# Raw weight tiles in the empty places of the next block's tokens, and roots of the norms on VectorE, in a hybrid decoder step

## Chip, cores and metric

One core of a Trainium2 chip runs the whole step. The metric is the device time of one execution in microseconds; the time before is the median of three runs.

## What is computed

One layer for 2048 prompt tokens and 64 sample tokens (8 sequences of 8) with D = 1024. The sample tokens attend to a paged cache of 8192 positions each. Cut to what matters here:

```python
h = rmsnorm(x, norm1_g)
b, c, u, q, k, v = project(h, w_in)
y_conv, new_conv = short_conv(b, c, u, conv_state, conv_w)
o = attend(q, k, v, lam)
...
x = x + jnp.concatenate([y_conv, o], axis=-1) @ w_out
h2 = rmsnorm(x, norm2_g)
x = x + jnp.square(jax.nn.relu(h2 @ w_up)) @ w_down
...
y_prompt = rmsnorm(xp, final_g)
y_sample = rmsnorm(xs, final_g)
```

`rmsnorm` divides by the root of a row's mean square. Everything is float32; a product is made of three matmuls on high and low parts.

## The kernel before

Five instruction streams are written in one program order by hand; each engine works through its own part of it in that order, and SP's and GpSimd's queues issue transfers in order too. There are three stages: the input projection (to about 640 us), the prompt's attention with the convolution and the first output projection (to about 1180 us), and the stage that the change is about: output projection and MLP. The decode attention of the sample tokens (gathers of `kraw` and `vpg` on GpSimd's queue, transposes `kt` on VectorE, small matmuls) is dealt out in steps between the matmuls until about 2640 us.

In the third stage the prompt's tokens come in four blocks of 384 (`Dense` objects in `ds`, three tiles of 128 tokens each), and a fifth block holds the 64 sample tokens and the last 512 prompt tokens in five tiles. `Dense.run` (L1454) works through one block: the first four up chunks (`first_ups`), then a loop over `c`: a down product of two weight tiles (`down`, L1400), a `poll()`, and two up chunks (`up`, L1377), each followed by a `poll()`. There are NC = 16 such chunks. Near the end it calls the next block's `out_proj` (L1313 is its add of x) between its last two down products, so that blocks overlap. `poll` (L2085) takes one entry from the list `rest`; `before_last` empties that list and loads the mixed activations of the next block.

Weights stream through `Weights` (L204): `load` issues a tile of 512 KB into a raw buffer `wr` of two; `split` makes `wh` on ScalarE (L227) and `wl` on VectorE (L229), four buffers each, and then loads the next raw tile. So two raw tiles are on their way, and a raw load is issued when the one two before it has been split. TensorE reads `wh` and `wl` alone.

Tokens of block i stand in three places `x1_(i mod 2)0..2` of the pool `xb`. They are read from HBM by `load_x` (L1243), get both residual adds there (L1313, L1418), and leave by `final` (L1441). So the three places of the other parity are empty from the last `final` of a block to the next `load_x` into them. In the kernel before, the second block's tokens are loaded by the first polls of the first block on SP's queue; those of the third and fourth block by the polls after a block's outputs, on GpSimd's queue.

Norms: `norm_sum` (L272) squares and sums a row on ScalarE (`junk`, L277). `norm_root` (L280) makes the root in ten steps on one column, two of them integer steps that always run on VectorE (L287, L288), the others on the engine that is passed. `Dense` passes `self.eng`, which EN1 and ENG set to GpSimd. It is used in `norm_early` (L1273), in front of `scale` (which makes `xn`, L1256) and `turn` (tps, h2h, h2l), and in `final` (in front of y, L1450), where GpSimd's queue also sends y out. The first output projection, inside attention, passes GpSimd by itself (L1692). In the input projection `prep_root` (L357) does the same for three rows at once by `rsqrt` (L137), and L474 passes GpSimd.

Of the kernel before, what the change touches and what calls it, by code (L numbers as in the profile page):

```python
# [8 lines left out]
F32 = mybir.dt.float32  # L9
# [9 lines left out]
P = 128  # L19
# [2 lines left out]
LAM0 = 0.8 - 0.6  # L22
RATES = (0.8, 0.45, 0.8)
BURST = (3, 2, 1, 0)
ENG = True
MO = (5, 2, 1, 0, 0)
ST = 0
OW = 3
# [21 lines left out]
KUP = True  # L50
DA = 2
SHR = 0
EN1 = True
DW = 20.0
GP2 = (2, 1, 2, 3, 2, 2, 3, 3)
GP = (3, 2, 1, 3, 2, 2, 3, 3)
# [6 lines left out]
NDS = 4  # L63
# [4 lines left out]
def tile_hymba_step(  # L68
# [7 lines left out]
    nc = tc.nc  # L76
# [127 lines left out]
    class Weights:  # L204


        def __init__(self, pool, srcs, raw_bufs, bufs, share=0):
            self.share = share
            self.pool, self.srcs, self.rb, self.b = pool, srcs, raw_bufs, bufs
            self.raw, self.out, self.nr, self.ns, self.ng = {}, {}, 0, 0, 0  # L210
            self.parts_left = 0

        def load(self, upto):
            while self.nr < min(upto, len(self.srcs)):
                src = self.srcs[self.nr]
                t = self.pool.tile([P, 1024], F32, tag="wr", bufs=self.rb, name="wraw")
                dma(out=t.rearrange("p (k f) -> p k f", k=src.shape[1]), in_=src)
                self.raw[self.nr] = t
                self.nr += 1

        def split(self, upto):
            while self.ns < min(upto, len(self.srcs)):
                self.load(self.ns + 1)
                t = self.raw.pop(self.ns)
                wh = self.pool.tile([P, 1024], F32R, tag="wh", bufs=self.b, name="wh")
                wl = self.pool.tile([P, 1024], F32R, tag="wl", bufs=self.b, name="wl")
                nc.scalar.copy(wh, t)  # L227
                eng = nc.gpsimd if self.share and dec["gen"] is not None and self.ns % self.share == 1 else nc.vector
                eng.tensor_sub(wl, t, wh.bitcast(F32))  # L229
                k = self.srcs[self.ns].shape[1]  # L230
                self.out[self.ns] = (wh.rearrange("p (k f) -> p k f", k=k), wl.rearrange("p (k f) -> p k f", k=k))
                self.ns += 1
                self.load(self.ns + self.rb)

        def parts(self):

            if self.ns == len(self.srcs):
                return []
            i, box = self.ns, {}
            self.ns += 1  # L240
            self.parts_left = 4
            self.load(i + 1)

            def high(h):
                if h == 0:
                    box["t"] = self.raw.pop(i)
                    box["h"] = self.pool.tile([P, 1024], F32R, tag="wh", bufs=self.b, name="wh")
                    box["l"] = self.pool.tile([P, 1024], F32R, tag="wl", bufs=self.b, name="wl")
                nc.scalar.copy(box["h"][:, 512 * h:512 * h + 512], box["t"][:, 512 * h:512 * h + 512])
                self.parts_left -= 1  # L250

            def low(h):
                c = slice(512 * h, 512 * h + 512)
                nc.vector.tensor_sub(box["l"][:, c], box["t"][:, c], box["h"][:, c].bitcast(F32))
                self.parts_left -= 1
                if h == 1:
                    k = self.srcs[i].shape[1]
                    self.out[i] = tuple(box[x].rearrange("p (k f) -> p k f", k=k) for x in "hl")
                    self.load(i + 1 + self.rb)

            return [lambda: high(0), lambda: high(1), lambda: low(0), lambda: low(1)]

# [88 lines left out]
    def prep_stats(bi, ci):  # L351
        ss = prep_sums(bi, ci)
        for i in range(len(chunks[bi][ci])):
            prep_sum(bi, ci, ss, i)
        return ss

    def prep_root(bi, ci, ss, eng=None):  # L357
        rr = small.tile([P, 8], F32, tag="nrr", name="rr")
        w = len(chunks[bi][ci])
        nc.vector.tensor_scalar(ss[:, 0:w], ss[:, 0:w], EPS, None, op0=ALU.add)  # L360
        rsqrt(rr, ss, P, w, eng)
        return rr

    def prep_scale(bi, ci, rr):

        def f(i):
            x, n = xt[bi, ci][i], chunks[bi][ci][i][2]
            nc.vector.scalar_tensor_tensor(x[:n], x[:n], rr[:n, i:i + 1], g1[:n], op0=ALU.mult, op1=ALU.mult)
        return [lambda i=i: f(i) for i in range(len(chunks[bi][ci]))]
# [75 lines left out]
    cs = {}  # L445

    class Proj:


        def __init__(self, bi, mi):  # L450
# [20 lines left out]
            if mi == len(order) - 8 and bi + 1 < len(blocks):  # L471
                prep_load(bi + 1, 0)
            if mi == len(order) - 6 and bi + 1 < len(blocks):
                cs["scale"] = prep_scale(bi + 1, 0, prep_root(bi + 1, 0, prep_stats(bi + 1, 0), nc.gpsimd))  # L474
            if bi == 0 and mi == 8:
                cs["consts"] = conv_consts()
            if bi == 0 and mi == 10:
# [634 lines left out]
    for j in range(1, 4 * H):  # L1112
        h, g = divmod(j, 4)
# [47 lines left out]
    NC = NF // CH  # L1161
# [27 lines left out]
    class Dense:  # L1189
# [261 lines left out]
                                               op0=ALU.mult, op1=ALU.mult)  # L1451
                eng.dma_start(out=dst[r0:r0 + n, :], in_=y[:n])

        def run(self, ub, poll, before_last, nxt, after):  # L1454
            self.ub = ub
            self.first_ups()
            for c in range(NC - 2):
                self.down(range(c * CH, (c + 1) * CH))
                poll()
                ms = range((c + 2) * CH, (c + 3) * CH)  # L1460
                if c < NC - 3:
                    for m in ms:
                        self.up(m)
                        poll()
            w = []
            if len(self.groups) == 1 and KUP:

                w = [W.get() for m in ms]
                pss = [psA.tile([P, 512], F32, tag="a", name="ups")[:, 0:self.nt] for m in ms]
                for g in range(2):  # L1470
                    for i in range(len(ms)):
                        if 2 * g + i == HU:
                            dec["hold"] = True
                        self.up_rows(pss[i], w[i], 0, range(4 * g, 4 * g + 4))
                        if i == 0:
                            W.ahead(1 + g)
                    before_last(g)
                for ps, m in zip(pss, ms):
                    self.up_out(ps, m, 0)
                W.ahead(WL)  # L1480
            else:

                for gi in range(len(self.groups)):
                    for i, m in enumerate(ms):
                        if gi == 0:
                            w.append(W.get())
                            W.ahead(2)
                        self.up_chunk(m, gi, w[i])
                W.ahead(3)
            if after is None:  # L1490
                self.down(range((NC - 2) * CH, (NC - 1) * CH))
                nxt().out_proj()
                self.down(range((NC - 1) * CH, NF))
            else:
                self.down(range((NC - 2) * CH, NF), after)
# [569 lines left out]
    dec["paused"] = False  # L2065
    burst(BURST[1])
    box = {}
    rest = [lambda ti=ti: ds[1].load_x(ti) for ti in range(3)]

    def switch():  # L2070

        if box or dec["gen"] is not None:
            return
        dec["close"]()
        dctx.close()
        sm = ctx.enter_context(tc.tile_pool(name="mlp_sm", bufs=1, side="right", reuse_waits="tile"))
        slots = xslots(NDS) + [(sm, f"x1_{ti}") for ti in range(3, 5)]
        t0 = 384 * NDS
        d = Dense([[(xs, ys, 0, NS)] + ptiles(t0, t0 + 256), ptiles(t0 + 256, T)], sm, slots, ENG and nc.gpsimd)
        box["d"] = d  # L2080
        box["todo"] = [lambda gi=gi, x=x, g=g: d.load_mix(gi, [g], x)
                       for gi in range(2) for g in range(2) for x in "hl"]
        box["todo"] += [lambda ti=ti: d.load_x(ti) for ti in list(range(3, 5)) + list(range(3))]

    def poll():  # L2085
        switch()
# [5 lines left out]
    def before_last(g):  # L2092
        while rest:
            rest.pop(0)()
        if cur[0] < NDS - 1:
            ds[cur[0] + 1].load_mix(0, [g])
            return
        drain()
        switch()
        while box["todo"]:  # L2100
            box["todo"].pop(0)()

    cur = [0]
    for i, d in enumerate(ds):
        cur[0] = i
        d.run([(sb1, "uh", "ul", 4, 384)], poll, before_last, lambda: ds[cur[0] + 1] if cur[0] < NDS - 1 else box["d"], None)
        rest += [lambda: load_gain("f", nc.gpsimd)] + FN * [lambda: None]
        for ti in range(4):
            rest += [lambda d=d, ti=ti: d.final(ti, nc.gpsimd), lambda: None]
        if i < NDS - 1:  # L2110
            rest.append(lambda: load_gain("2", nc.gpsimd))
        if i < NDS - 2:
            rest += [lambda i=i, ti=ti: ds[i + 2].load_x(ti, nc.gpsimd) for ti in range(3)]
    c1.close()
    psA = ctx.enter_context(tc.tile_pool(name="mlp_psA2", bufs=8, space=PSUM, reuse_waits="tile"))
    sb2 = ctx.enter_context(tc.tile_pool(name="mlp_sb2", bufs=1, reuse_waits="tile"))
# [37 lines left out]
```

## Time and profile before

| what | value |
|---|---|
| time, median of three runs (lowest to highest) | 3207.14 us (3206.44 to 3207.63) |
| the profiled execution | 3218.23 us, of it the span 3216.5 us |
| busy share of the span | TensorE 95%, VectorE 59%, ScalarE 41%, GpSimd 28% |
| DMA | 624.7 MB, mean 194 GB/s |

The span is counted from the first to the last instruction. The page cuts it into 40 slices: TensorE is at nine tenths or more in nearly all from the third on, and its granted clock shows nine tenths or more in every slice. The DMA digits are highest, 5 to 8, where decode and MLP run together, and 2 after decode has ended.

### The profile page before, as it was taken

To read this page: it belongs to the slowest core of one execution; us is meant where nothing else is said; L and a number is where in the kernel's file an instruction comes from. 1 tells how busy PE (TensorE), PEld (TensorE's weight loads), DVE (VectorE), ACT (ScalarE), POOL (GpSimd) and SP (SyncE) were. 2 spreads that over 40 slices of the span, in tenths; PEclk is the share of its full clock that TensorE was granted. 3 is DMA by queue.
4 is the path that set the end of the run, shared out by engine and by line. 5 is a ranking of instruction groups with operands and counts; after the bars stand their busy time and mean duration, and the time that the engine had idled before them with its cause. 6 is when DMAs were issued, how large, how long until landed. Compare 5 with 4: busy or idle time off the path is not lost.

```text
span 3216.5 us, 55392 instructions
## 1 busy us (share of the span) xinstructions
PE 3046.2 (95%) x21670; PEld 2597.1 (81%) x21670; DVE 1905.9 (59%) x3861; ACT 1334.1 (41%) x2873; POOL 896.5 (28%) x1274
## 2 busy tenths in 40 slices
PE   7998998999999999998999999999989999999998
PEld 7997877989997888876777767777767888788887
DVE  5465344268888667765667656666556554454454
ACT  3323323357778643342343424333333433333333
POOL 1012353311222120133554344544335430110001
PEclk9999999999999999999999999999999999999999
DMA  5666875854335356676787786787757756232222
GB/s 156 220 222 217 287 255 164 258 142 111 105 102 147 128 169 209 221 233 236 249 284 271 239 289 220 258 285 267 279 189 254 230 181 201 74 101 81 79 79 76
DMA packets 443295, 624.74 MB, mean 194 GB/s; under 512 B 36661, under 2 KB 337717, under 8 KB 426650
## 3 DMA queue, kind: packets, MB, share of 16 engines
q1 hardware_dynamic: 378730, 335.68, 33.9%
q0 software_dynamic: 63136, 282.11, 24.8%
q8 instruction: 171, 2.80, 0.4%
q10 hardware_dynamic: 1168, 3.41, 0.3%
q14 instruction: 90, 0.74, 0.1%
HBM read 565.35 MB, written 55.74 MB: 193 GB/s over the span
## 4 chain that ended last, share of the span: by engine, by line
PE 74%; DVE 8%; issue 5%; DMA 5%; ACT 4%; POOL 3%; another core or an unknown queue 1%; SPq 0%; ACTq 0%; POOLq 0%; DVEq 0%
PE ups L200 7%; PE ups L202 7%; PE ups L201 6%; PE dps L1411 6%; PE dps L1412 6%; PE dps L1413 6%; PE ps L200 6%; PE ps L202 5%; PE ps L201 5%; PE asc L1833 3%; PE o_ps L950 3%; PE sps L903 3%; PE O L1920 3%; DMA wraw<-in_w_out_dram 2%; DVE kt L718 2%
## 5 line engine op out<-in xcount | busy, mean ns | idle before, releaser
L229 DVE TENSOR_TENSOR wl<-wraw,wh 128x1024 fp32r<-128x1024 f32 x408 | 498.3, 1222 | 325.5 <-ACT wh L227 245.4
L227 ACT CAST wh<-wraw 128x1024 fp32r<-128x1024 f32 x408 | 425.7, 1049 | 578.7 <-PE dps L1413 179.6
L708 POOL DMA_INDIRECT vpg<-in_cache_v_dram,pt x512 | 537.7, 1050 | 329.5 <-PE o_ps L950 155.4
L200 PE MATMUL ups<-h2h,wh 128*128 128x384 f32 (+2 forms) x1520 | 503.9, 332 | 9.7 <-DVE x L1418 7.7
L202 PE MATMUL ups<-h2h,wl 128*128 128x384 f32 (+2 forms) x1520 | 490.8, 323 | 1.0 <-DVE wl L229 1.0
L201 PE MATMUL ups<-h2l,wh 128*128 128x384 f32 (+2 forms) x1520 | 489.3, 322 | 0.1
L1412 PE MATMUL dps<-wl,uh 128*128 128x512 f32 (+1 forms) x1076 | 428.1, 398 | 26.2 <-DVE wl L229 24.8
L1411 PE MATMUL dps<-wh,uh 128*128 128x512 f32 (+1 forms) x1076 | 439.3, 408 | 9.6 <-DVE x L1313 3.4
L1418 DVE TENSOR_TENSOR x<-dps,x 128x512 f32<-128x512 f32 (+1 forms) x534 | 355.5, 680 | 136.3 <-PE dps L1413 120.3
L1413 PE MATMUL dps<-wh,ul 128*128 128x512 f32 (+1 forms) x1076 | 425.1, 395 | 0.0
L200 PE MATMUL ps<-hh,wh 128*128 128x384 f32 (+1 forms) x1152 | 406.0, 352 | 2.7 <-issue 1.6
L202 PE MATMUL ps<-hh,wl 128*128 128x384 f32 (+1 forms) x1152 | 377.2, 327 | 3.1 <-DVE wl L229 2.5
L201 PE MATMUL ps<-hl,wh 128*128 128x384 f32 (+1 forms) x1152 | 377.2, 327 | 1.2 <-issue 1.1
L700 POOL DMA_INDIRECT kraw<-in_cache_k_dram,idxk x128 | 127.3, 994 | 862.3 <-DVE kt L718 824.9
L1370 DVE TENSOR_TENSOR ul<-r,uh 128x384 fp32r<-128x384 f32 (+2 forms) x190 | 100.3, 528 | 385.3 <-ACT uh L1369 350.2
L200 PEld LDWEIGHTS ups<-h2h,wh 128*128 128x128 f32 x1520 | 286.4, 188 | 45.1 <-issue 38.0
L718 DVE STREAM_TRANSPOSE kt<-kraw 128x512 f32<-128x512 f32 x512 | 317.7, 677 | 0.0
L201 PEld LDWEIGHTS ups<-h2l,wh 128*128 128x128 f32 x1520 | 286.7, 189 | 2.3
L202 PEld LDWEIGHTS ups<-h2h,wl 128*128 128x128 f32 x1520 | 286.1, 188 | 2.2 <-DVE wl L229 1.8
L1367 ACT ACTIVATE r<-ups 128x384 f32<-128x384 f32 (+2 forms) x190 | 88.2, 464 | 440.6 <-PE ups L202 341.5
L1411 PEld LDWEIGHTS dps<-wh,uh 128*128 128x128 f32 (+1 forms) x1076 | 201.3, 187 | 80.9 <-issue 26.5
L1412 PEld LDWEIGHTS dps<-wl,uh 128*128 128x128 f32 (+1 forms) x1076 | 201.9, 188 | 72.6 <-DVE wl L229 34.4
(275 smaller groups left out, 4843.4 us busy)
## 6 DMA issues: line engine op xcount, KB each, us to landing
wraw<-in_w_up_dram SPq DMA_DIRECT2D x160, 512.0 KB
wraw<-in_w_down_dram SPq DMA_DIRECT2D x160, 512.0 KB
wraw<-in_w_in_dram SPq DMA_DIRECT2D x72, 512.0 KB
wraw<-in_w_out_dram SPq DMA_DIRECT2D x40, 512.0 KB
x<-in_x_prompt_dram SPq DMA_DIRECT2D x21, 512.0 KB
vpg<-in_cache_v_dram,pt POOLq DMA_INDIRECT x512
qt<-QH SPq DMA_DIRECT2D x64, 128.0 KB
qt<-QL SPq DMA_DIRECT2D x64, 128.0 KB
```

Of the source, the lines that this page charges most:

```text
L200: nc.tensor.matmul(ps, lhsT=wh, rhs=ah, start=first, stop=False)
L201: nc.tensor.matmul(ps, lhsT=wh, rhs=al, start=False, stop=False)
L202: nc.tensor.matmul(ps, lhsT=wl, rhs=ah, start=False, stop=last)
L227: nc.scalar.copy(wh, t)
L229: eng.tensor_sub(wl, t, wh.bitcast(F32))
L700: nc.gpsimd.indirect_dma_start(out=t.rearrange("p a b -> p (a b)"), out_offset=None, in_=ck, in_offset=bass.IndirectOffsetOnAxis(ap=idxk[: ...
L708: nc.gpsimd.indirect_dma_start(out=t[:, g, :], out_offset=None, in_=cv, in_offset=bass.IndirectOffsetOnAxis(ap=idxv[:, 4 * it + g:4 * it + ...
L718: nc.vector.transpose(t[:, e, 16 * j:16 * j + 16].rearrange("p a b -> p (a b)"), kraw[2 * r + e][:, 16 * j:16 * j + 16].rearrange("p a b - ...
L1411: nc.tensor.matmul(ps, lhsT=uh, rhs=wh[:, half], start=(i == 0), stop=False)
L1412: nc.tensor.matmul(ps, lhsT=uh, rhs=wl[:, half], start=False, stop=False)
L1413: nc.tensor.matmul(ps, lhsT=ul, rhs=wh[:, half], start=False, stop=(i == len(ms) - 1))
L1418: nc.vector.tensor_add(xx, ps, xx)
```

## The change

Two things are changed.

First, `Weights` can borrow places. `lend(slots)` adds places to `extra` and loads into them at once; `load` takes an own raw buffer if one is free, else a lent one; `back(i)`, called when tile i has been split, returns the place and loads up to 2 + 3 tiles ahead; `take_back` ends the loan. In block i the places of the next block's three tokens' tiles are lent: at the first poll in the first block, in the others by an entry of `rest` behind the outputs. `run` takes them back after the down product of c = NC - 7 = 9 and, after that of c = 11, calls `x_loads`, which puts the next block's three token loads into `rest`, now on SP's queue for every block. The loads that stood at the first polls and on GpSimd's queue are gone. The fifth block's first three tiles are loaded in `before_last`, where they stood already in effect.

Second, EN1 and ENG are False, so `norm_root` in `Dense` runs all its steps on VectorE; and the `prep_root` at the end of a projection block does so too. The roots of the first output projection (L1692 before) and those of attention stay on GpSimd.

```diff
-ENG = True
+ENG = False
...
-EN1 = True
+EN1 = False
...
+            self.own, self.extra, self.held = raw_bufs, [], {}
...
+        def lend(self, slots):
+
+            self.lent = list(slots)
+            self.extra += slots
+            self.load(len(self.srcs))
+
+        def take_back(self):
+
+            self.lent, self.extra = [], []
+
+        def back(self, i):
+
+            slot = self.held.pop(i, None)
+            if slot is None:
+                self.own += 1
+            elif slot in self.lent:
+                self.extra.append(slot)
+            self.load(i + 1 + self.rb + len(self.lent))
...
-            while self.nr < min(upto, len(self.srcs)):
+            while self.nr < min(upto, len(self.srcs)) and (self.own or self.extra):
                 src = self.srcs[self.nr]
-                t = self.pool.tile([P, 1024], F32, tag="wr", bufs=self.rb, name="wraw")
+                if self.own:
+                    self.own -= 1
+                    t = self.pool.tile([P, 1024], F32, tag="wr", bufs=self.rb, name="wraw")
+                else:
+                    slot = self.held[self.nr] = self.extra.pop(0)
+                    t = slot[0].tile([P, 1024], F32, tag=slot[1], name="wraw")
...
-                self.load(self.ns + self.rb)
+                self.back(self.ns - 1)
...
-                cs["scale"] = prep_scale(bi + 1, 0, prep_root(bi + 1, 0, prep_stats(bi + 1, 0), nc.gpsimd))
+                cs["scale"] = prep_scale(bi + 1, 0, prep_root(bi + 1, 0, prep_stats(bi + 1, 0)))
...
                 poll()
+                if c == NC - 7:
+                    W.take_back()
+                if c == NC - 5:
+                    x_loads()
...
-    rest = [lambda ti=ti: ds[1].load_x(ti) for ti in range(3)]
+    rest = []
+
+    def lend(i):
+
+        rest.append(lambda: W.lend([(xb, f"x1_{(i + 1) % 2}{ti}") for ti in range(3)]))
+
+    def x_loads():
+        while rest:
+            rest.pop(0)()
+        assert not W.held
+        nxt = ds[cur[0] + 1] if cur[0] < NDS - 1 else None
+        if nxt:
+            rest.extend(lambda ti=ti: nxt.load_x(ti) for ti in range(3))
+
+    lend(0)
...
-        if i < NDS - 2:
-            rest += [lambda i=i, ti=ti: ds[i + 2].load_x(ti, nc.gpsimd) for ti in range(3)]
+        if i < NDS - 1:
+            lend(i + 1)
```

Lines shift by 27 behind `Weights`, and by more behind. GpSimd's order in the third block, where the second block's outputs are made (L285 to L292 are a root, L708 and L700 gathers, L1452 sends y); before:

```order
L708 DMA vpg<-in_cache_v_dram,pt 128x512 x8
L700 DMA kraw<-in_cache_k_dram,idxk 128x2048
L285 TENSOR_SCALAR ss<-ss 128x1
L286 TENSOR_SCALAR ss<-ss 128x1
L290 TENSOR_SCALAR ss<-ss 128x1
L292 TENSOR_SCALAR ss<-ss 128x1
L290 TENSOR_SCALAR ss<-ss 128x1
L292 TENSOR_SCALAR ss<-ss 128x1
L290 TENSOR_SCALAR ss<-ss 128x1
L292 TENSOR_SCALAR rr<-ss 128x1
L1452 DMA out_dram<-y 128x1024
L700 DMA kraw<-in_cache_k_dram,idxk 128x2048
```

and the same place in the changed kernel (L735 and L727 are the gathers, L1479 sends y):

```order
L735 DMA vpg<-in_cache_v_dram,pt 128x512 x8
L727 DMA kraw<-in_cache_k_dram,idxk 128x2048
L1479 DMA out_dram<-y 128x1024
L727 DMA kraw<-in_cache_k_dram,idxk 128x2048
L735 DMA vpg<-in_cache_v_dram,pt 128x512 x8
```

The root between the gathers is gone; the queue holds gathers and sends alone.

VectorE's order at the same place (y is the scaled output, wl is the low part of a weight tile); before:

```order
L287 TENSOR_SCALAR ss<-ss 128x1
L288 TENSOR_SCALAR ss<-ss 128x1
L1450 SCALAR_TENSOR_TENSOR y<-x_0_13312,rr,gain 128x1024
L229 TENSOR_TENSOR wl<-wraw,wh 128x1024
L718 STREAM_TRANSPOSE kt<-kraw 128x512 x3
```

and changed:

```order
L312 TENSOR_SCALAR ss<-ss 128x1
L313 TENSOR_SCALAR ss<-ss 128x1
L314 TENSOR_SCALAR ss<-ss 128x1
L315 TENSOR_SCALAR ss<-ss 128x1
L317 TENSOR_SCALAR ss<-ss 128x1
L319 TENSOR_SCALAR ss<-ss 128x1
L317 TENSOR_SCALAR ss<-ss 128x1
L319 TENSOR_SCALAR ss<-ss 128x1
L317 TENSOR_SCALAR ss<-ss 128x1
L319 TENSOR_SCALAR rr<-ss 128x1
L1477 SCALAR_TENSOR_TENSOR y<-x_0_15171,rr,gain 128x1024
L256 TENSOR_TENSOR wl<-wraw,wh 128x1024
```

The root stands where its two integer steps stood, with eight more steps, ahead of y and of the next `wl`.

Token loads: before, those of the fourth block on GpSimd's queue, behind the outputs of the second block:

```order
L708 DMA vpg<-in_cache_v_dram,pt 128x512 x8
L1506 DMA gain<-in_norm_g_dram 128x1024
L1247 DMA x_0_21472<-in_x_prompt_dram 128x1024
L700 DMA kraw<-in_cache_k_dram,idxk 128x2048
L1247 DMA x_1_21565<-in_x_prompt_dram 128x1024
L700 DMA kraw<-in_cache_k_dram,idxk 128x2048
L1247 DMA x_2_21618<-in_x_prompt_dram 128x1024
L708 DMA vpg<-in_cache_v_dram,pt 128x512 x8
L700 DMA kraw<-in_cache_k_dram,idxk 128x2048 x2
```

and in the changed kernel on SP's queue, between the raw tiles of the twelfth and thirteenth chunk:

```order
L130 DMA wraw<-in_w_up_dram 128x8x128 x2
L130 DMA wraw<-in_w_down_dram 128x1024 x2
L130 DMA wraw<-in_w_up_dram 128x8x128
L1274 DMA x_0_23169<-in_x_prompt_dram 128x1024
L130 DMA wraw<-in_w_up_dram 128x8x128
L1274 DMA x_1_23230<-in_x_prompt_dram 128x1024
L130 DMA wraw<-in_w_down_dram 128x1024 x2
L1274 DMA x_2_23324<-in_x_prompt_dram 128x1024
L130 DMA wraw<-in_w_up_dram 128x8x128 x2
L130 DMA wraw<-in_w_down_dram 128x1024 x2
```

They moved from one queue to the other, and from the fifth chunk of a block to its twelfth.

## Rows read from the trace of the kernel before

**Rows 1.** the page's first line

```profile
span 3216.5 us, 55392 instructions
```

**Rows 2.** busy time by stretch; behind the engines granted clock, DMA share, GB/s

```profile
1180.00:2790.00 1610.00, 1528.43 (x11149) 1228.88 (x11148) 998.80 (x1671) 599.12 (x1053) 592.33 (x689) 0.98 0.70 236
1593.05:1599.87 6.82, 4.02 (x20) 1.93 (x21) 4.32 (x7) 2.05 (x3) 5.41 (x10) 0.50 0.89 295
2453.20:2456.62 3.42, 3.42 (x18) 2.12 (x11) 1.55 (x2) 2.28 (x6) 2.59 (x6) 0.50 0.78 253
1511.13:1514.54 3.41, 3.41 (x12) 2.47 (x10) 2.75 (x4) 1.29 (x3) 2.13 (x4) 0.50 0.20 50
2767.23:2777.47 10.24, 7.66 (x26) 6.08 (x27) 6.93 (x11) 1.75 (x3) 3.10 (x8) 0.50 0.33 103
2115.28:2122.11 6.83, 6.23 (x42) 4.25 (x43) 3.20 (x5) 1.04 (x1) 5.31 (x6) 0.50 0.94 294
```

**Rows 3.** TensorE's waits, 1180 to 2790 us: who for whom, us, times, longest

```profile
PE dps L1412 <- DVE wl L229: 23.8, 16, 4.7
PE ps L1301 <- DVE wl L229: 11.9, 9, 4.3
...
PE tps L1268 <- DVE x L1418: 5.8, 4, 1.8
PE tps L1268 <- DVE h2l L1271: 5.1, 3, 1.9
PE dps L1411 <- DVE x L1313: 3.4, 3, 1.1
```

**Rows 4.** waits over the whole span; the last line counts GpSimd's roots (source line L285)

```profile
POOL ss L285 <- ACT junk L277: 543.8, 21, 296.8
...
DVE ss L287 <- POOL ss L285: 55.7, 25, 6.5
...
DVE xn L1256 <- POOL rr L292: 28.5, 15, 2.5
...
L285 POOL TENSOR_SCALAR ss<-ss x33: 208/219/433, 1125.5 to 3204.1; 128x1 f32<-128x1 f32 x31, 64x1 f32<-64x1 f32 x2
```

**Rows 5.** timeline of TensorE: start, us, instruction, [idle before <-releaser]

```profile
1595.85 0.80 PE L1412 MATMUL dps<-wl,uh 128*128 128x512 f32 x1 [4.74 <-DVE wl L229]
...
2452.09 0.50 PE L1412 MATMUL dps<-wl,uh 128*128 128x512 f32 x1 [2.54 <-DVE wl L229]
```

**Rows 6.** timeline of VectorE in front of four gaps of TensorE

```profile
1593.13 0.15 DVE L287 TENSOR_SCALAR ss<-ss 128x1 int32<-128x1 int32 x1 [4.45 <-POOL ss L285]
...
2018.51 0.15 DVE L287 TENSOR_SCALAR ss<-ss 128x1 int32<-128x1 int32 x1 [4.91 <-POOL ss L285]
...
2038.09 0.15 DVE L287 TENSOR_SCALAR ss<-ss 128x1 int32<-128x1 int32 x1 [3.70 <-POOL ss L285]
...
2449.36 0.15 DVE L287 TENSOR_SCALAR ss<-ss 128x1 int32<-128x1 int32 x1 [4.48 <-POOL ss L285]
```

**Rows 7.** timeline of GpSimd at the first of them

```profile
1592.86 0.24 POOL L285 TENSOR_SCALAR ss<-ss 128x1 f32<-128x1 f32 x1
```

**Rows 8.** timeline of VectorE at the kernel's end: a root of its own

```profile
3204.31 0.15 DVE L287 TENSOR_SCALAR ss<-ss 128x1 int32<-128x1 int32 x1 [1.59 <-POOL ss L285]
...
3207.47 0.69 DVE L1418 TENSOR_TENSOR x<-dps,x 128x512 f32<-128x512 f32 x1 [1.02 <-PE dps L1413]
...
3209.47 0.15 DVE L285 TENSOR_SCALAR ss<-ss 128x1 f32<-128x1 f32 x1
...
3211.46 0.21 DVE L292 TENSOR_SCALAR rr<-ss 128x1 f32<-128x1 f32 x1
```

**Rows 9.** timelines of GpSimd, ScalarE and TensorE in the third block of tokens

```profile
2084.74 0.57 POOL L1247 DMA_DIRECT2D x<-in_x_prompt_dram  x1
...
2104.15 1.05 ACT L227 CAST wh<-wraw 128x1024 fp32r<-128x1024 f32 x1 [10.23 <-DMA wraw<-in_w_up_dram]
...
2115.88 0.80 PE L1412 MATMUL dps<-wl,uh 128*128 128x512 f32 x1 [2.42 <-DVE wl L229]
```

More of the change, by code (lines that the diff above doesn't have):

```diff
@@ L210, in __init__ @@
             self.raw, self.out, self.nr, self.ns, self.ng = {}, {}, 0, 0, 0
+            self.own, self.extra, self.held = raw_bufs, [], {}
             self.parts_left = 0
+        def lend(self, slots):
[11 more added lines that the diff above has]
+            self.load(i + 1 + self.rb + len(self.lent))
+        lent = []
         def load(self, upto):
-            while self.nr < min(upto, len(self.srcs)):
+            while self.nr < min(upto, len(self.srcs)) and (self.own or self.extra):
                 src = self.srcs[self.nr]
-                t = self.pool.tile([P, 1024], F32, tag="wr", bufs=self.rb, name="wraw")
+                if self.own:
[4 more added lines that the diff above has]
+                    t = slot[0].tile([P, 1024], F32, tag=slot[1], name="wraw")
                 dma(out=t.rearrange("p (k f) -> p k f", k=src.shape[1]), in_=src)
@@ L258, in low @@
                     self.out[i] = tuple(box[x].rearrange("p (k f) -> p k f", k=k) for x in "hl")
-                    self.load(i + 1 + self.rb)
+                    self.back(i)
             return [lambda: high(0), lambda: high(1), lambda: low(0), lambda: low(1)]
@@ L1452, in final, with run @@
                 eng.dma_start(out=dst[r0:r0 + n, :], in_=y[:n])
-        def run(self, ub, poll, before_last, nxt, after):
+        def run(self, ub, poll, before_last, nxt, after, x_loads=lambda: None):
             self.ub = ub
@@ L2082, in switch @@
                        for gi in range(2) for g in range(2) for x in "hl"]
-        box["todo"] += [lambda ti=ti: d.load_x(ti) for ti in list(range(3, 5)) + list(range(3))]
+        box["todo"] += [lambda ti=ti: d.load_x(ti) for ti in range(3, 5)]
     def poll():
@@ L2101, in before_last @@
             box["todo"].pop(0)()
+        if g == 0:
+            for ti in range(3):
+                box["d"].load_x(ti)
     cur = [0]
@@ L2105, in tile_hymba_step @@
         cur[0] = i
-        d.run([(sb1, "uh", "ul", 4, 384)], poll, before_last, lambda: ds[cur[0] + 1] if cur[0] < NDS - 1 else box["d"], None)
+        d.run([(sb1, "uh", "ul", 4, 384)], poll, before_last, lambda: ds[cur[0] + 1] if cur[0] < NDS - 1 else box["d"], None, x_loads)
         rest += [lambda: load_gain("f", nc.gpsimd)] + FN * [lambda: None]
```

## Prediction

> **What bounds the kernel now.** TensorE does. I read the page first, then busy time by stretch, then TensorE's waits, then the timelines of the engine that each wait names. The change reaches the stage after attention, from 1180 us to the end. In the 1610 us of it that decode shares, TensorE is busy for 1528.4, so 81.6 us are idle, and the granted clock is 0.98 [rows 2]. All that this change can win there is a part of these 81.6 us and of the time at half clock. The largest wait is of the down projection on split weights, 23.8 us in 16 times; the output projection waits 11.9 us for the same; the turning of a new block's tokens (tps) and the bank it needs wait 5.8 + 5.1 + 3.4 = 14.3 us [rows 3].
>
> Why are split weights late? Two of the four longest of these waits are 4.74 and 2.54 us [rows 5]; the other two, of 4.66 and 2.27 us, lie between them and look alike, 14.2 us together. In front of each, VectorE stands still for 4.45, 4.91, 3.70 and 4.48 us, because the integer step of a root (L287) waits for GpSimd's first step (L285) [rows 6]. GpSimd is not slow at it, it is late: it starts that step at 1592.86 only [rows 7], since gathers stand ahead of it on its queue, though VectorE has been free since 1593.13 - 4.45 = 1588.68. The subtraction that makes `wl` is queued behind the root and y, and TensorE stands until it is done. [...]
>
> **Part 1, four roots on the output side (gain 13.9 us).** A root on VectorE costs 3211.46 + 0.21 - 3209.47 = 2.2 us [rows 8]. Two of its ten steps (0.3 us) were there already, so 1.9 us are added. The squares end before VectorE is free in three of the four cases and 0.2 us after it in one, so VectorE reaches y earlier by its wait less 1.9: 2.5, 2.8, 1.8 and 2.5 us, 9.6 of the 14.2 us. Three stretches at half clock follow these gaps, 6.8, 6.8 and 3.4 us (first and last in rows 2), 17.1 us that cost 8.5; shorter gaps should spare half, 4.3. Bounds: nothing, and all of it, 14.2 + 8.5 = 22.7. I take 9.6 + 4.3 = 13.9.
>
> [...]
>
> **Part 2, the other 26 roots (gain 8 us).** GpSimd does 33 roots [rows 4]; three at the first output projection stay there, 30 move. Fourteen of these stand in the passage from one block to the next (three tails of three tokens' tiles, one of five), sixteen with the outputs. VectorE waits for GpSimd 55.7 + 28.5 = 84.2 us in all [rows 4]. Less the four of part 1 (17.5) and the share of the three that stay (84.2 x 3/33 = 7.7), 59 us remain, and the 26 roots cost 26 x 1.9 = 49.4. So VectorE gains 9.6 us net, some 2.4 per tail; I give TensorE 8 of them, since in the tails its 14.3 us of waits [rows 3] are for xn, h2l and x, which stand in VectorE's queue right behind these roots. Upper bound: all 14.3, and the half of the low-clock stretches of the four tails, 3.4 us three times and 10.2 once (first and last in rows 2), 10.2: together 24.5. Lower bound: no wait falls and each of the 14 costs 1.9, a loss of 26.6. The range between them is wide; the value stays near the net freed time. GpSimd loses eight steps per root and six loads of tokens; nobody waits for it there any more, and its gathers are bounded by their buffers.
>
> The two roots of three columns in the projection go the same way: about 2 us each of VectorE, which is not the late engine there, and the scaling that uses them comes some 5 us later. I take 0 (bounds 0 and 3.8).
>
> **Part 3, the lent places (gain 5 us).** They are lent from the first chunk of the first block, but in the later ones only after the outputs' twelve steps, three per chunk: from the fourth chunk's end to the tenth. The output projection, where 11.9 us of TensorE's waits for weights lie [rows 3], comes after they are taken back and gains nothing. Within the loans I find one weight-bound place, in the third block: ScalarE waits 10.23 us for a raw tile, TensorE 2.42 us, and 6.8 us at half clock follow [rows 2, 9]: 2.4 + 3.4 = 5.8. Bounds 0 and 5.8; I take 5.
>
> **Part 4, tokens loaded later (loss 6 us).** The 1.5 MB of the next block's tokens now come in the twelfth and thirteenth chunk, on SP's queue, where raw tiles of weights with two in flight again stand behind them. They were just what the late tile of part 3 met: one token load is issued at 2084.74, the next some 4 us later, just ahead of that tile [rows 9]. That happened in one block of three. I charge it once, 6 us; bounds 0 and 3 x 5.8 = 17.4. The last block's tokens stay where they were.
>
> **Part 5, the end (loss 0.9 us).** The last root but one takes 1.9 us longer from 3204.31; VectorE had 1.02 us of rest before 3207.47 [rows 8], so 0.9 us reach the end. Bounds 0 and 1.9.
>
> **Part 6, what is late next (loss 4 us).** Where VectorE comes earlier, the raw tile is the next to be late, as in the output projection today; I take a third of its 11.9 us, with bounds 0 and 11.9.
>
> Sum: -13.9 - 8 - 5 + 6 + 0.9 + 4 = -16.0 us against the profiled execution of 3218.2 us (span 3216.5 [rows 1]), so 3202.2. That execution is 11.1 us above the median of the runs; the same 16.0 off 3207.1 give **3191.1, say 3191 us**.
>
> **The rivals.** *Loads come next* (0.16): GpSimd only hid that two raw tiles in flight are too few. For it: the loan is closed in the first chunks, where the four gaps are. Against: the raw tiles of these gaps had been cast before VectorE went on. Then parts 1 and 3 come back as waits for DMA, and -8 + 6 + 0.9 leave -1: 3206. *VectorE becomes the bound* (0.13), the other sign: in 21 of the 33 roots GpSimd was idle until ScalarE's squares were done [rows 4], so VectorE cannot begin these sooner, and it holds up `wl`, h2l and x for 1.9 us more each. Parts 1 and 3 less 4 and 5 are worth 13.9 + 5 - 6.9 = 12; from the seventh root whose 1.9 us TensorE pays, the kernel is slower; at twelve it is 23 - 12 = 11 us slower, 3218. Against: VectorE waits for GpSimd's result a second time in the tails, 28.5 us, which goes altogether. *Tokens collide in every block* (0.05): part 4 is 17.4, the sum -4.6, 3202.5. *The tails open* (0.08): part 2 is 24.5, which gives 3174.6. That the loan does nothing at all costs only part 3, 3196, and is inside my forecast.
>
> **The numbers.** My forecast, a gain of about 16 us, has 0.58. About 0.2% (6.4 us) is what a measurement of this kernel can tell from no change. Faster: 0.58 + 0.08 = 0.66; same: 0.16 + 0.05 = 0.21; slower: 0.13. The low end, 3168, has part 1 whole (another 8.8) and most of part 2's bound (14 more). The high end, 3213, takes in the first and third rival and the milder half of the second.
>
> **What would show it.** Right: no wait of VectorE's root for GpSimd between 1500 us and the end; the four gaps of TensorE under 2.3 us and fewer stretches at 0.50; GpSimd with some 240 steps fewer; no 10 us wait of ScalarE for a raw tile in the third block's loan; the tokens' loads on SP near the twelfth chunk, and one weight wait of some 2 us behind them. Wrong: TensorE's waits on h2l, xn and x in the tails grow past 14.3 us (the second rival), or its waits on `wl` stay at 23.8 us with ScalarE waiting for DMA in front of them (the first). If both fall and the time does not, I have missed what bounds the stage.

## The result and the profile after

The changed kernel takes 3176.2 us (median of four runs, 3170.2 to 3178.6) against 3207.1: a ratio of 0.9901, 95% interval 0.9885 to 0.9916, so **31 us less, 27 to 37**. Forecast were 16 us less. The profiled execution of after is the one of 3178.6 us.

The first lines of its page answer to [rows 1]: VectorE has 260 steps more than before, GpSimd 272 fewer.

```profile
span 3176.7 us, 55329 instructions
...
PE 3024.5 (95%) x21670; PEld 2590.5 (82%) x21670; DVE 1956.6 (62%) x4121; ACT 1334.2 (42%) x2873; POOL 779.9 (25%) x1002
```

TensorE's waits from 1180 to 2760 us (who for whom, us, times, longest) answer to [rows 3]:

```profile
PE ps L1328 <- DVE wl L256: 13.4, 10, 5.0
PE dps L1439 <- DVE wl L256: 13.1, 15, 2.3
PE ups L200 <- DVE x L1445: 8.1, 4, 2.8
...
PE ups L200 <- ACT wh L254: 4.5, 1, 4.5
PE tps L1295 <- DVE h2l L1298: 4.4, 2, 2.2
PE ups L202 <- DVE wl L256: 3.9, 2, 2.1
```

The down projection waits 13.1 us for split weights where it waited 23.8; the output projection waits 13.4 us, 11.9 before. Two waits have come up: the up products (ups) wait 4.5 us for ScalarE's high part, which they did not before, and 3.9 us for `wl`, 1.0 before. TensorE's timeline shows where (answers to [rows 5]; start, us, instruction, idle before it):

```profile
1560.13 0.66 PE L200 MATMUL ups<-h2h,wh 128*128 128x384 f32 x1 [4.52 <-ACT wh L254]
1587.76 0.41 PE L200 MATMUL ups<-h2h,wh 128*128 128x384 f32 x1 [2.26 <-DVE x L1445]
1595.49 0.45 PE L202 MATMUL ups<-h2h,wl 128*128 128x384 f32 x1 [1.76 <-DVE wl L256]
1613.86 0.41 PE L1011 MATMUL ops<-osum,osc 128*128 128x32 f32 x2 [1.69 <-DVE osc L1008]
1995.24 0.51 PE L1439 MATMUL dps<-wl,uh 128*128 128x512 f32 x1 [1.81 <-DVE wl L256]
2411.18 0.50 PE L1439 MATMUL dps<-wl,uh 128*128 128x512 f32 x1 [1.43 <-DVE wl L256]
```

Of the four gaps of part 1, two are gone and two are left at 1.81 and 1.43 us. But in the first chunks of the second block, where one of 4.74 us stood, there are now four, 10.2 us together. ScalarE's timeline names what is late there:

```profile
1557.09 1.04 ACT L254 CAST wh<-wraw 128x1024 fp32r<-128x1024 f32 x1 [10.43 <-DMA wraw<-in_w_up_dram]
...
1584.70 1.05 ACT L254 CAST wh<-wraw 128x1024 fp32r<-128x1024 f32 x1 [9.25 <-DMA wraw<-in_w_up_dram]
...
1609.98 1.05 ACT L254 CAST wh<-wraw 128x1024 fp32r<-128x1024 f32 x1 [4.13 <-DMA wraw<-in_w_up_dram]
```

It is the raw tile in three of the four: the first gap follows the first of these casts, and the second and fourth follow steps of VectorE (the addition to x, and osc of the decode attention) that stand behind the `wl` of the other two. No loan is open there yet. The third gap has no late tile; VectorE is at its transposes of `kt` (3.08 us from 1588.81) and other decode steps until 1593.62. The first gap lies ahead of the block's first output (y at 1572.58), and the profiles with the outputs' roots on GpSimd have one of 1.2 to 3.7 us there too, so the change did not make it. The total is good, but part 1 did not come about as forecast, and the loan is suspect of more than its 5 us.

### The profile page after: what moved, and what is told of

Its sections match the earlier page's. It is cut to its first block, busy times and chain, and to the rows that moved or that the text cites. A ratio compares the mean times of both kernels' runs of the same rounds, so it can differ in the third digit from the quotient of the medians.

```text
span 3176.7 us, 55329 instructions
## 1 busy us (share of the span) xinstructions
PE 3024.5 (95%) x21670; PEld 2590.5 (82%) x21670; DVE 1956.6 (62%) x4121; ACT 1334.2 (42%) x2873; POOL 779.9 (25%) x1002
## 4 chain that ended last, share of the span: by engine, by line
PE 70%; DVE 10%; DMA 9%; issue 5%; ACT 3%; POOL 3%; SPq 0%; ACTq 0%; DVEq 0%; POOLq 0%
PE ups L200 7%; PE dps L1438 6%; PE ups L202 6%; PE ups L201 6%; PE dps L1439 6%; PE dps L1440 6%; PE ps L200 5%; PE ps L202 5%; PE ps L201 5%; PE asc L1864 4%; DMA wraw<-in_w_up_dram 3%; PE O L1951 3%; PE sps L930 3%; PE o_ps L977 3%; DVE kt L745 2%
## 5 line engine op out<-in xcount | busy, mean ns | idle before, releaser
L735 POOL DMA_INDIRECT vpg<-in_cache_v_dram,pt x512 | 533.6, 1042 | 323.8 <-PE o_ps L977 178.6
L1445 DVE TENSOR_TENSOR x<-dps,x 128x512 f32<-128x512 f32 (+1 forms) x534 | 356.2, 681 | 114.8 <-PE dps L1440 114.1
L727 POOL DMA_INDIRECT kraw<-in_cache_k_dram,idxk x128 | 125.6, 982 | 938.9 <-DVE kt L745 922.4
L1438 PEld LDWEIGHTS dps<-wh,uh 128*128 128x128 f32 (+1 forms) x1076 | 200.2, 186 | 75.6 <-issue 23.8
```

Of the source, the lines that this page charges most:

```text
L735: nc.gpsimd.indirect_dma_start(out=t[:, g, :], out_offset=None, in_=cv, in_offset=bass.IndirectOffsetOnAxis(ap=idxv[:, 4 * it + g:4 * it + ...
L1438: nc.tensor.matmul(ps, lhsT=uh, rhs=wh[:, half], start=(i == 0), stop=False)
L1445: nc.vector.tensor_add(xx, ps, xx)
```

## The experiments

The experiments ran on two chips (1 to 4 on one, 5 to 12 on the other) where the kernel before takes 3227 to 3237 us, not the 3207 of the first result; each is compared with runs of the kernel before on its own chip. Below, microseconds are the ratio less one, times 3232 us, with the 95% interval.

**1. Only the two roots of the projection on VectorE.** The first two profiles part by 16.4 us before the output projection begins, where I had charged 0.

```diff
-   ... prep_root(bi + 1, 0, prep_stats(bi + 1, 0), nc.gpsimd))
+   ... prep_root(bi + 1, 0, prep_stats(bi + 1, 0)))
```

> The kernel before, with one edit: the two roots of the input projection (three columns each) run on VectorE. Theory A (the projection gave 18 of the 31 us, because there GpSimd's root at 458.84 us stood and waited 6.5 us for VectorE with gathers queued behind it, and TensorE later waited for these gathers' tiles): 11 to 18 us less than before, about 3192, and the two traces part between 430 and 580 us. Theory B (the prediction's value for this step was right, and the 18 us between the two profiled executions are scatter of the one of before, which is 11 us above its median): within 2 us of before.

Measured 0.9995 (0.9978 to 1.0011): 1.6 us less, between 7 less and 4 more. Theory A falls.

**2. Only the thirty roots behind attention.**

```diff
-ENG = True
+ENG = False
-EN1 = True
+EN1 = False
```

> The kernel before, with the thirty roots behind attention on VectorE and nothing else: no loan, the projection's two roots on GpSimd. By the prediction's sum (parts 1, 2, 5 and 6): 13.9 + 8 - 0.9 - 4 = 17 us less than before, 3190. If the projection gave most of the change (theory A), what is left for roots and loan together is about 13 us, and this run gives 5 to 13 us. If the roots outside the third block cost as much as they free, 3 us or less.

Measured 0.9972 (0.9954 to 0.9990): 9 us less (3 to 15), half of the 17.

**3. All 32 roots, no loan** (the edits of 1 and 2 together).

> The whole change without the loan: all 32 roots that the change moves on VectorE, tokens loaded where they were before. If the loan is worth what the prediction took (5 gained, 6 lost): within 2 us of the changed kernel, 3175 to 3178. If it is the loan that closed the gap of the third block: 5 to 8 us slower than the changed kernel, 3182 to 3184. If loan and roots need each other (raw tiles are next to be late where VectorE comes earlier): 10 us or more slower than the changed kernel.

Measured 0.9972 (0.9952 to 0.9993): 9 us less (2 to 15). The changed kernel gains 26 to 31 (experiments 6 and 9, and the first result), so the loan carries the larger half. By size this is the third case, but its reason is not needed: these 9 us and the loan's 15 alone (experiment 4) make 24.

**4. Only the loan:** the changed kernel with ENG and EN1 True again and the projection's roots on GpSimd.

> The loan alone: the raw weights in the lent places and the tokens loaded in the twelfth chunk, all roots where they were before. The prediction's parts 3 and 4: -5 + 6, within 2 us of before. If the loan closes the third block's gap and the tokens meet nothing: 5 to 6 us less than before. If the later tokens collide in every block: 10 us more than before.

Measured 0.9954 (0.9935 to 0.9973): **15 us less** (9 to 21). None of the three cases has this; the prediction's two terms for the loan came to 1 us more.

**5 and 6. The kernel before and the changed kernel again, unchanged.**

> The kernel before, unchanged, for a second profile of it. The four runs so far were made on a chip whose median for the kernel before is 3237 us, 30 us above that of the first result. If the 18 us between the two first profiles in the projection (371 to 580 us) belong to the chip and not to the change, this profile has the projection as late as the four runs have it, whose TensorE was busy for 101 to 103 of the 109 us from 371 to 480 us, and not for 109.0 as in the first profile of the changed kernel.

> The changed kernel, unchanged, beside the parts. If roots (9 us less in the run of the norms) and loan (14 us less) simply add: 23 us less than before. If they need each other, as VectorE's earlier start makes the raw tile the next to be late: 30 us or more less, as in the first result (31). If the first result was made by its chip: 15 us less or fewer.

The profile of before has its first addition of the output projection at 1086.0 us (TensorE busy 103.3 of 109 us from 371 to 480), that of the changed kernel at 1084.1. In the first pair it was 1081.5 and 1065.1. The changed kernel's ratio is 0.9906 (0.9879 to 0.9932): 30 us less (22 to 39), without those 16 us of the projection. The interval holds the 23 us of a plain sum and the 31 of the first result. All twelve profiles of the experiments lie between 1079 and 1095 us there, with either kind of root: on these two chips that part is not the change's. What made the projection shorter in the first profile of after alone is left open, and so is whether the first chip's other runs share it.

**7. Only the later tokens:** experiment 4, with nothing lent.

```diff
-        rest.append(lambda: W.lend([(xb, f"x1_{(i + 1) % 2}{ti}") for ti in range(3)]))
+        rest.append(lambda: None)
```

> The kernel before with the tokens of the next block loaded in the twelfth and thirteenth chunk and nothing lent; roots as before. The prediction's part 4: up to 17 us more than before, 6 taken. If the loan's 14 us came from the places themselves: 0 to 6 us more than before. If they came from taking the tokens' 1.5 MB out of the first chunks, where they stood between the raw tiles, and the lent places do nothing: 10 to 14 us less than before.

Measured 0.9984 (0.9966 to 1.0003): 5 us less, between 11 less and 1 more, which lies between the cases. The later tokens cost nothing that shows; by the difference to experiment 4 the places themselves bring the rest, about 10 us (1 to 18, from two chips). ScalarE's waits for raw up weights (1180 to 2820 us) show what they do, first without, then with the lent places:

```profile
ACT wh L227 <- DMA wraw<-in_w_up_dram: 126.0, 49, 10.4
```

```profile
ACT wh L254 <- DMA wraw<-in_w_up_dram: 149.7, 51, 10.0
```

```profile
ACT wh L254 <- DMA wraw<-in_w_up_dram: 46.0, 23, 9.3
```

These are the kernel before (experiment 5), the later tokens (7) and the loan (4): 80 to 104 us of waiting of ScalarE go with the places. Single profiles scatter here: over all of them this sum is 126 to 166 us in the seven without the places and 46 to 103 us in the seven with them. It is clearest in chunks 5 to 10 of the third block, where the loan is open: ScalarE waits 33 to 60 us for raw tiles there in the seven profiles without the places, and less than 1 us in the seven with them.

**8. Only the sixteen roots of the outputs.**

```diff
-  self.rr[ti] = norm_root(norm_sum(self.x1[ti], n), n, self.eng)
+  self.rr[ti] = norm_root(norm_sum(self.x1[ti], n), n)
```

> The kernel before with sixteen of the thirty roots on VectorE, those of the outputs; the fourteen in the passages from block to block stay on GpSimd. By the prediction's part 1, these hold the four gaps: 14 us less than before, and the other fourteen bring little. If the roots' 9 us are those of the passages (the prediction's part 2): 2 us or less. If outputs' roots are worth more than 9, the passages' roots cost time.

Measured 1.0003 (0.9984 to 1.0022): **1 us more, between 5 less and 7 more**. So part 1 is worth nothing here, and by the difference to experiment 2, on the other chip, the fourteen of the passages bring about 10 us (2 to 18). VectorE's waits from 1180 to 2820 us suggest how that can be: first the kernel before (experiment 5), then this one.

```profile
DVE wl L229 <- ACT wh L227: 140.2, 94, 9.0
...
DVE ss L287 <- POOL ss L285: 34.0, 14, 6.5
```

```profile
DVE wl L229 <- ACT wh L227: 160.0, 96, 8.7
...
DVE ss L287 <- POOL ss L285: 18.6, 9, 6.5
```

VectorE waits 15.4 us less for GpSimd and 19.8 us more for `wh`, and ScalarE waits for raw up weights in turn:

```profile
ACT wh L227 <- DMA wraw<-in_w_up_dram: 166.1, 59, 10.7
```

It was 126.0. But these sums alone do not show it: with no loan and the outputs' roots on GpSimd, four profiles have 126 to 160 us of this wait, and the three with them on VectorE 144 to 166. TensorE's gap at 1591 us is 2.06 us (4.15 in experiment 5), and a new one of 1.76 us on `ups<-wl` stands 20 us behind it. That the wait is moved from one engine to another is seen below, place by place.

**9 to 11. The changed kernel again, and with one half of its roots back on GpSimd;** first the outputs', then the passages'.

```diff
-  self.rr[ti] = norm_root(norm_sum(self.x1[ti], n), n, self.eng)
+  self.rr[ti] = norm_root(norm_sum(self.x1[ti], n), n, nc.gpsimd)
```

```diff
-  self.rr[ti] = norm_root(ss, n, self.eng)
+  self.rr[ti] = norm_root(ss, n, nc.gpsimd)
```

> The changed kernel once more, on the chip of the three runs beside it, as their measure. If the first result and the run before hold: 28 to 32 us less than before.

> The changed kernel with the sixteen roots of the outputs back on GpSimd; loan, tokens and the passages' fourteen roots as changed. Alone these sixteen gave nothing (1 us more than before, interval 5 less to 7 more): TensorE's four gaps shrank, and ScalarE's waits for raw tiles grew in their place. If they are worth nothing beside the loan as well: as the changed kernel, within 3 us. If the lent places are what lets them pay, as the raw tile is then there when VectorE comes earlier: 8 to 14 us slower than the changed kernel.

> The changed kernel with the fourteen roots of the passages from block to block back on GpSimd; loan, tokens and the outputs' roots as changed. By the difference of the runs of thirty and of sixteen roots, these fourteen are worth 10 us: 8 to 12 us slower than the changed kernel. If that difference was scatter: as the changed kernel, within 3 us.

| run | ratio to before | median, us |
|---|---|---|
| 9, as changed | 0.9921 (0.9893 to 0.9949) | 3206.9 |
| 10, outputs on GpSimd | **0.9886 (0.9861 to 0.9911)** | 3191.4 |
| 11, passages on GpSimd | 0.9934 (0.9911 to 0.9957) | 3209.7 |

Experiment 9 is 26 us less than before (17 to 35), just short of the 28 to 32 expected. Both answers of experiment 10's expectation are wrong: with the outputs' roots back on GpSimd the changed kernel is *faster*. All runs from 5 on are of one chip, so I take the twelve runs of the changed kernel together (experiments 6 and 9, mean 3203.0): experiment 10 (mean 3192.0) is 11.0 us below, 95% interval 4 to 18; experiment 11 (mean 3210.0) is 7 us above, between 1 below and 15 above, which does not decide between its two answers. **Experiment 10 beats both kernels**: 37 us less than before (29 to 45).

The four gaps of part 1 are not what it gains: they stand in experiment 10 as in the kernel before (4.97, 3.71, 2.50 and 3.95 us), and TensorE's waits of the down projection for `wl` from 1180 to 2820 us, 24.3 us in experiment 5, are

```profile
PE dps L1439 <- DVE wl L256: 23.5, 14, 5.0
```

Where this comes from can be seen by cutting the traces at the additions of the down products to x (L1418, or L1445; 96 in a block, six in a chunk). For each profile the table has the time between the same additions in every kernel: the four passages (from the first addition of a block's last chunk to the next block's first, summed), the second block's chunks 1 to 4, and chunks 5 to 10, the loan's, of the second and third block.

| profile | passages | 2nd, chunks 1-4 | 2nd, 5-10 | 3rd, 5-10 |
|---|---|---|---|---|
| before, two profiles | 150.4, 150.1 | 96.2, 95.1 | 137.9, 141.3 | 133.1, 135.7 |
| 1, projection's roots | 150.1 | 98.0 | 139.7 | 138.3 |
| 7, later tokens | 148.0 | 96.5 | 138.5 | 135.0 |
| 4, loan | 150.1 | 97.3 | 138.0 | 127.2 |
| 8, outputs' roots | 147.1 | 99.4 | 138.6 | 134.4 |
| 2, thirty roots | 144.2 | 100.4 | 139.1 | 138.3 |
| 3, all 32 roots | 143.2 | 102.5 | 140.1 | 135.9 |
| changed, three profiles | 141.3, 141.2, 142.6 | 104.3, 102.0, 100.6 | 131.2, 134.8, 134.7 | 127.2, 126.2, 127.2 |
| 11, no passages' roots | 148.8 | 101.7 | 134.7 | 127.2 |
| 10, no outputs' roots | 143.0 | 97.3 | 135.2 | 126.7 |
| 12, longer loan | 143.3 | 101.9 | 134.7 | 127.2 |

Each part has its column. The passages take 147 to 150 us with their roots on GpSimd, 141 to 144 with them on VectorE. The loan takes 6 to 12 us off the third block's chunks 5 to 10 and, in most profiles, some 4 off the second's; in the first and fourth block these chunks are as long with it as without (112.3 and some 122 us). And the outputs' roots on VectorE *lengthen* the second block's first chunks, where the first gap of part 1 lay, from 95 to 98 us to 99 to 104. In the third and fourth block, where the other three gaps lay, chunks 1 to 4 are on average as long with the roots on either engine (96.2 us on GpSimd and 96.3 on VectorE; 93.0 and 92.9). So of the 11 us of experiment 10 the traces place some 5 in the second block; another 3 are in the fifth block with the end (406.9 us in experiment 10, 409.7 to 409.8 in the three profiles of the changed kernel), and the rest has no place in them.

The reason for the second block's part stands on GpSimd's queue. First experiment 10, the outputs' root on GpSimd: its timelines of GpSimd, SP and ScalarE.

```profile
1588.22 2.67 POOL L317 TENSOR_SCALAR ss<-ss 128x1 f32<-128x1 f32 x1 [0.28 <-issue]
...
1594.04 1.02 POOL L735 DMA_INDIRECT vpg<-in_cache_v_dram,pt  x1 [0.30 <-issue]
...
1582.81 7.96 SPq L130 DMA_DIRECT2D wraw<-in_w_up_dram  x2
...
1593.23 1.05 ACT L254 CAST wh<-wraw 128x1024 fp32r<-128x1024 f32 x1 [4.55 <-DMA wraw<-in_w_up_dram]
```

Now the same place in the changed kernel (experiment 9), which comes to it some 7 us later:

```profile
1594.14 0.95 POOL L735 DMA_INDIRECT vpg<-in_cache_v_dram,pt  x1 [0.30 <-issue]
1595.10 0.58 POOL L1479 DMA_DIRECT2D out_dram<-y  x1
1596.44 0.98 POOL L735 DMA_INDIRECT vpg<-in_cache_v_dram,pt  x1 [0.76 <-PE dps L1440]
...
1590.50 5.30 SPq L130 DMA_DIRECT2D wraw<-in_w_up_dram  x2
...
1603.48 1.05 ACT L254 CAST wh<-wraw 128x1024 fp32r<-128x1024 f32 x1 [5.53 <-DMA wraw<-in_w_up_dram]
...
1608.01 1.05 ACT L254 CAST wh<-wraw 128x1024 fp32r<-128x1024 f32 x1 [3.48 <-DMA wraw<-in_w_up_dram]
```

With the root on GpSimd, the send of y comes 10.3 us after the first raw up tile was issued (1593.12 - 1582.81) and the next four gathers of V pages 11.2 us after it, and that tile is cast 10.4 us after its issue: before either. Without the root the send comes 4.6 us and the gathers 5.9 us after the issue (1596.44 - 1590.50), in the middle of the tile's way, and the cast comes after 13.0 us, of which ScalarE waits the last 5.5.

All fourteen profiles show this at the first output of the second block, and the two kinds do not overlap. With the outputs' roots on GpSimd (six profiles) the gathers start 11.0 to 11.3 us after the tile's issue, the cast 10.0 to 10.9 us after it, and ScalarE waits 3.0 to 5.1 us. With them on VectorE (eight) these are 5.5 to 5.9, 12.9 to 15.7 and 5.4 to 9.3 us. What the transfers did in the 10.4 us behind the issue, first in experiment 10, then in 9 (q0 has GpSimd's transfers, q1 SP's; packets, MB, share of the DMA engines):

```profile
q0 software_dynamic: 464, 2.10, 58.1%
q1 hardware_dynamic: 1671, 0.94, 29.9%
```

```profile
q0 software_dynamic: 543, 2.40, 69.3%
q1 hardware_dynamic: 1202, 0.79, 24.4%
```

GpSimd's queue moves 0.3 MB more and SP's 0.15 MB less. Over all the profiles, in the first 10 us behind the issue, q0 moves 2.09 to 2.10 MB and q1 0.82 to 0.93 with the roots on GpSimd, 2.23 to 2.41 and 0.68 to 0.79 with them on VectorE. The slow root held transfers back; when they come earlier, they share the DMA engines with the raw tile. Which of them matter is not shown. The 512 KB of y stand on the queue in front of the four gathers, so y is a rival to them; no run moved the one without the other.

**12. A longer loan,** each place lent as soon as it is empty, taken back one chunk later, and the three roots of the first output projection, the last ones left on GpSimd behind attention, on VectorE.

```diff
-            self.lent = list(slots)
+            self.lent = self.lent + list(slots)
...
-                if c == NC - 7:
+                if c == NC - 6:
                     W.take_back()
-                if c == NC - 5:
+                if c == NC - 4:
                     x_loads()
...
-            rest += [lambda d=d, ti=ti: d.final(ti, nc.gpsimd), lambda: None]
+            rest.append(lambda d=d, ti=ti: d.final(ti, nc.gpsimd))
+            if i < NDS - 1 and ti >= 2:
+                lend(i + 1, [ti - 2])
...
-            d.rr[ti] = norm_root(ss.pop(ti), P, nc.gpsimd)
+            d.rr[ti] = norm_root(ss.pop(ti), P)
```

> The changed kernel with a longer loan: each place is lent as soon as its own tile's output is made (one or two steps earlier for the first two), taken back one chunk later, the tokens loaded one chunk later; and the three roots at the first output projection also on VectorE. If the waits for raw tiles outside the loan still cost time: 3 to 6 us less than the changed kernel. If the tokens now come too late for the passage: TensorE's wait on x there grows by 2 us or more in each of three blocks, and the kernel is 5 us or more slower. If neither: within 3 us.

Measured 0.9901 (0.9876 to 0.9927), median 3196.5: 5 us below the mean of the changed kernel's twelve runs, between 12 below and 1 above. That fits the first case without deciding it, and three things change at once. The tokens were not too late: the four passages take 143.3 us.

## Why the prediction was right, and where not

The sign and the range held: 3176 us lies between 3168 and 3213. The size was half, and the terms were further off than their sum. That the total stayed in the range is in part luck: the loan, forecast with its tokens as a loss of 1 us, gave the larger half, and the outputs' roots, forecast as a gain of 9, gave nothing.

| step | forecast, us | measured, us |
|---|---|---|
| part 1, outputs' roots (with 5 and 6) | -13.9 + 0.9 + 4 | +1 alone (-5 to 7); +11 beside the rest (4 to 18) |
| part 2, passages' roots | -8 | -10 (run 2 less run 8; -18 to -2); -7 beside the rest (-15 to 1) |
| part 2, the projection's roots | 0 | -1.6 (-7 to 4) |
| parts 3 and 4, loan and tokens | -5 + 6 | -15 (-21 to -9) |

*Part 1 failed.* Its step was that VectorE "reaches y earlier by its wait less 1.9", and that TensorE gains those 9.6 us. VectorE did come earlier, and the four gaps did shrink, as forecast. But in the second block the next raw tile was then late (cast 12.9 to 15.7 us after its issue and not 10.0 to 10.9) and cost more than the gap there; in the third and fourth block the same chunks became no shorter, and why the smaller gaps bring nothing there is left open. For the second block the first rival, *Loads come next*, describes the outputs' roots. I set it aside because "the raw tiles of these gaps had been cast before VectorE went on"; true of these tiles, not of the ones behind. Part 6 priced just this, at 4 us; it ate all of part 1. The other wrong sentence is in part 2: of GpSimd without the roots I said that "its gathers are bounded by their buffers". They, and the sends of y, were also held by the roots that they stood behind, and when these went, they came earlier, among the raw tiles. The second rival's price, 1.9 us of VectorE per root, did not decide it at the place shown, where VectorE stands idle for 5.4 us in front of the late tile's `wl`, though its sign is right for these sixteen. The price itself holds: a root of the changed kernel takes 2.2 us (1570.46 to 1572.66).

*Part 2 was right* in size and place: the four passages together take 141 to 144 us in every profile with their roots on VectorE and 147 to 150 in every one without, some 6 us, and TensorE's waits for the turning of new tokens (tps) did not grow (13.8 us before, 9.8 after). The projection's 0 holds.

*Part 3 was mis-sized:* 5 forecast for the third block alone, 6 to 12 measured there and some 4 in the second. I priced the places within the loans where TensorE waited long for a raw tile, and the profile of before shows one. The second profile of before has the same gap (2.41 us at 2118), so this was no accident, but it is not all: other profiles without the places have more (up to five over 1 us in this stretch, in experiment 1), and ScalarE waited 38.0 us for raw tiles there in the first profile, of which I priced one wait, 10.23. With the places none of this is left.

*Part 4 charged a collision that cost nothing* the runs can show (run 7: 5 us less, between 11 less and 1 more). Its premise, that the tokens made the tile of part 3 late, is weak too: with the tokens gone from there and nothing lent (run 7), ScalarE still waits 7.5 us for the same tile. The forecast wait behind the later loads is there, but small: in the changed kernel's first profile the raw tile issued between two of them is late for ScalarE, and TensorE waits 2.08 us for a step of VectorE that stands behind the `wl` of this tile (SP, ScalarE and TensorE):

```profile
2212.72 1.12 SPq L1274 DMA_DIRECT2D x<-in_x_prompt_dram  x1
2215.67 0.38 SPq L130 DMA_DIRECT2D wraw<-in_w_up_dram  x1
...
2226.24 1.05 ACT L254 CAST wh<-wraw 128x1024 fp32r<-128x1024 f32 x1 [5.23 <-DMA wraw<-in_w_up_dram]
...
2229.45 0.41 PE L1011 MATMUL ops<-osum,osc 128*128 128x32 f32 x2 [2.08 <-DVE osc L1008]
```

That the tile is late because of the loads is not shown. The wait of 1.70 us for `wl` just before, at 2214, is not theirs: its tile was cast at 2209.26, before the first of them, and VectorE was at its transposes of `kt`, 1.89 us from 2212.18; this `wl` starts at 2214.43.

*Part 5 holds:* from the integer step of the last root but one to the end it is 12.8 us (below), 12.2 before [rows 1, 8]; 0.6 more, 0.9 forecast.

```profile
3163.94 0.15 DVE L314 TENSOR_SCALAR ss<-ss 128x1 int32<-128x1 int32 x1
```

Of the signs named beforehand, no root of VectorE waits for GpSimd between 1500 us and the end; the four gaps are under 2.3 us; and ScalarE's 10 us wait in the third block's loan is gone. The stretches at half clock (0.50) from 1170 to 2790 us are as many as before, 13, and shorter, 61.4 us together and 71.7 before. In such a stretch of the kernel before the matmuls of the down product start 0.43 us apart (2454.82 to 2456.53), behind it 0.23 (2456.81 to 2457.50): by this the 10.3 us less are worth some 5, an estimate. That shorter gaps spared them, part 1's 4.3 us, no run shows. Most signs came true in a kernel in which part 1 gave nothing: they follow the named waits, not the one that takes their place.

What stays open: the parts do not add up. Run 10 gains 37 us, where loan (15) and passages' roots (10) alone make 25; the intervals are wide enough for chance, and no run separates them.

## What to carry to other kernels

When a wait is to be taken away, look at the next instruction of the same kind, not at the one that waited: here its input came from a queue with two transfers in flight, and the wait went there (5.4 to 9.3 us of ScalarE for the raw tile, where it was 3.0 to 5.1). The fastest kernel of this case keeps the four gaps, 2.50 to 4.97 us. The root in front of transfers on GpSimd's queue also spaced them: the send of y came 10.3 us after the raw tile's issue with it and 4.6 us without. Before such work is moved off, ask what the transfers will meet when they come earlier. And move it piece by piece: of these roots the passages' fourteen paid (10 us by runs 2 and 8), the outputs' sixteen cost (11 us beside the rest).

## What was not expected of the hardware

- A root with eight of its ten small steps on GpSimd, one of them 2.67 us where the other two of its line in the same root take 0.34, was better for this kernel at the outputs than 2.2 us on VectorE (experiment 10, 11.0 us below the changed kernel). At the second block's first output y was sent 10.3 and not 4.6 us after a raw tile's issue, the gathers behind it started 11.2 and not 5.9 us after it, and the tile was cast after 10.4 and not 13.0.
- The same kernel differs from chip to chip, or from one time to another: the kernel before took 3207 us in the first measurement and 3227 to 3237 on the two chips of the experiments, 0.6 to 0.9% more, and there its runs spread by 18 to 28 us where four runs of the first lay within 1.2 (its profiled execution was 11 us longer). Ratios agree (0.9901, 0.9906, 0.9921).
